# A hybrid decoder layer on one core: where the squares of rows stand in ScalarE's queue, which pool the first four weight chunks land in, and when the x rows by token are loaded

## The chip, the core and the metric

The kernel runs on one core of a Trainium2 chip. The metric is the device time of one execution in microseconds, as the median of several runs; lower is better. One further execution was recorded by the hardware profiler, and all single durations below are from that recording.

## The reference

One decoder layer over 256 tokens of width 2048, all in float32, with 256 memory tokens beside it:

```python
hn = rmsnorm(h, norm_mix_w)
q, k, v, g_ret, xr, yr, g_a, g_b = split(hn @ w_in)          # 2048 x 14336
ret_out = silu(g_ret) * head_groupnorm(chunkwise_retention(rotary(q), rotary(k), v))
rnn_out = gelu(yr) * rg_lru(causal_dwconv(xr))
merged = sigmoid(g_a) * (ret_out @ w_proj_ret) + sigmoid(g_b) * (rnn_out @ w_proj_rnn)
h = h + merged @ w_mix_out
mem_n = rmsnorm(mem, norm_mem_w)
h = h + memory_cross_attention(rmsnorm(h, norm_xa_w), mem_n, xa_w_q, xa_w_k, xa_w_v, xa_w_o)
h = h + conv_gated_ffn(rmsnorm(h, norm_ffn_w), ffn_w_up, ffn_w_down)   # width 5632
return rmsnorm(h, final_norm_w)
```

Each rmsnorm needs, for each token, the sum of squares over the 2048 features. The change concerns three of these sums (of x, of the memory rows, of h after each of the two residual additions) and the loads at the very start.

## The kernel before, in words

**Products.** Every weight matrix is cut into blocks of 512 columns, and each block into chunks of 4 row tiles of 128 (1 MB in float32); the first two blocks, of q and of v, are cut into chunks of 2, 2, 4, 4 and 4 row tiles that alternate (chunk 0 of q, chunk 1 of v, chunk 2 of q, and so on). Weights and activations are split into a rounded part `hi` and the rest `lo`, and a product is the sum of three matmuls. A full chunk takes 24 matmuls of 128x512; a chunk of `steps_t` has some of 128x256.

**The weight stream.** `weight_stream` lists all chunks in the order of use. `prefetch` (L233) takes them in that order, up to `AHEAD` = 2 chunks before their use: it issues the load of `raw` on SP's queue (L249), then for each half of the chunk a cast to `hi` on ScalarE, ACT in the profile (L276), and a subtraction to `lo` on VectorE, DVE (L277). `raw` has 3 buffers, `hi` and `lo` 6 each, that is three chunks. Chunks 0 and 1 are loaded in four single row tiles together, chunks 2 to 5 in pieces of two row tiles (512 KB), which I call 4a and 4b for chunk 4; later ones in one piece. Beside the first five chunks of q the transposed x comes in pairs of row tiles (`xt`, 256 KB a pair, L530), which `split_cols` scales and splits on ACT and DVE (L451, L452). x by token (`nat`, four loads of 512 KB, L228) is used for the sums of squares alone (L493), two rows when chunk 8 is taken and two at chunk 9.

**The order of work.** Most instructions are put into each engine's queue by a scheduler that works from priorities in program order; matmuls keep the program's order. Each queue then runs strictly in order. `later(n, fn)` puts a piece of code n + 1 chunks later in the program. Of SP's loads at most eight are under way at once: each waits for the landing of the eighth before it, besides what its buffer waits for.

**The big pool.** All larger tiles (rows, planes, splits, gates) take one of 27 buffers of 4 KB a partition, in turn, from `big`.

**Turning rows.** `by_dma` turns rows by token into rows by feature: two copies of half words into `pl` on ACT (L385), two DMA transposes on SP's queue into `pt` (L387), and, some chunks later, `join`: two copies from `pt` into `f` on ACT (L396), and what follows from `f`.

**The residual.** `residual` (L840) runs after `w_mix_out` and after `xa_w_o`. It makes four products (0 to 3), of four chunks each. The first three chunks of products 0 and 1 come first, then the last chunk of 0, the last of 1, and then products 2 and 3 whole. After each product, DVE adds it to the rows of h (L852), `squares` sums the squares of the new rows on ACT in two instructions (L867), and `by_dma` turns the rows; `turn` then splits `f` by `split_cols`. In the first residual, `memory_steps` hangs other work between the products: at block 1 the squares of the memory rows, `mnat` (four loads of 512 features each, two instructions a load, L493), and what makes `rsms` of them; at block 3 the loads of the transposed memory. The merged rows that feed the first residual are turned by the same `by_dma`; the join of the last of them comes four chunks after its gate product.

Of the kernel before, what the change touches and what calls it, by code (L numbers as in the profile page):

```python
# [9 lines left out]
F32 = mybir.dt.float32  # L10
# [7 lines left out]
P = 128  # L18
# [10 lines left out]
BW = 512  # L29
KC = 4  # L30
KH = 2
RAW_BUFS = 3
# [106 lines left out]
def hybrid_layer(  # L139
# [19 lines left out]
    wp = ctx.enter_context(tc.tile_pool(name="wp", bufs=2))  # L159
# [8 lines left out]
    def nm(s):  # L168
        count[0] += 1
        return f"{s}_{count[0]}"  # L170

    def big(shape, dt=F32, s="b"):
        return bp.tile(shape, dt, tag="big", name=nm(s))
# [11 lines left out]
    def load_rows(src, c, cs=slice(0, BW), t=None):  # L185

        if t is None:
            t = big([P, 2, BW], s="nat")
        rows = src[0].rearrange("(t p) d -> p t d", p=P)
        sp.dma_start(out=t[:, :, cs], in_=rows[:, :, c * BW + cs.start : c * BW + cs.stop])  # L190
        return t
# [31 lines left out]
    def load_x(n):  # L223
        while len(xin) < n:
            t = big([P, 2, BW], s="nat")
            rows = x[0].rearrange("(t p) d -> p t d", p=P)
            c = len(xin) * BW
            sp.dma_start(out=t, in_=rows[:, :, c : c + BW])  # L228
            xin.append(t)
# [3 lines left out]
    def prefetch(n):  # L233
        while len(ahead) < n and taken[0] < len(stream):
            i = taken[0]
            name, row, nk, c = stream[i]
            taken[0] += 1
            size = nk * P * BW
            src = wall[at[0] : at[0] + size].rearrange("(p k n) -> p k n", p=P, k=nk)
            at[0] += size  # L240
            raw = wp.tile([P, KC, BW], F32, tag="raw", bufs=RAW_BUFS, name=nm("raw"))
            k2 = row // (KH * P)
            early = i < 2 * len(EARLY)
            own = early and i % 2 == 0
            cuts = range(nk + 1) if i < 2 else range(0, nk + 1, KH) if i < 6 else (0, nk)
            if own:
                xs.load(k2 + 1)
            for a, b in zip(cuts, cuts[1:]):
                sp.dma_start(out=raw[:, a:b, :], in_=src[:, a:b, :])  # L249
                if i == 0 and a == 0:  # L250
                    sp.dma_start(out=xs.rest[0], in_=xs.rest[1])
                elif own and a == 0:
                    xs.load(k2 + nk // KH)
            if i >= 5:
                load_x(min(4, i - 4))
            if i == 8:
                sp.dma_start(out=cid, in_=consts[:, 0:C_DEC])
                sp.dma_start(out=pa[:, 16:P], in_=by_feature[:, 16:P])
                sp.dma_start(out=pb, in_=by_feature[:, P : P + 80])
            if i == 13:  # L260
                sp.dma_start(out=pf.rearrange("p a n -> p (a n)"), in_=by_feature[:, P + 80 :])
            if i in (8, 9):
                for b in (2 * i - 16, 2 * i - 15):
                    sum_squares(xin[b], ss0, b, pin=True)
            parts = []
            for k in range(0, nk, KH):
                if own:
                    xs[k2 + k // KH]
                hi = wp.tile([P, KH, BW], F32R, tag="hi", bufs=PART_BUFS, name=nm("hi"))
                lo = wp.tile([P, KH, BW], F32R, tag="lo", bufs=PART_BUFS, name=nm("lo"))  # L270
                for cs in (slice(k, k + 1), slice(k + 1, k + 2)) if i < 2 else (slice(k, k + KH),):
                    ds = slice(cs.start - k, cs.stop - k)
                    if i == 0:
                        dve.tensor_copy(hi[:, ds], raw[:, cs, :])  # L274
                    else:
                        act.copy(hi[:, ds], raw[:, cs, :])  # L276
                    dve.tensor_tensor(  # L277
                        out=lo[:, ds], in0=raw[:, cs, :], in1=hi[:, ds].bitcast(F32), op=ALU.subtract
                    )
                parts.append((hi, lo))  # L280
            ahead.append(((row, c), parts))
# [3 lines left out]
    def later(n, fn):  # L285

        pending.append((step[0] + n + 1, fn))
# [18 lines left out]
    def ended(steps):  # L306

        for a in steps:
            pass
        return a  # L310
# [41 lines left out]
    def steps_n(w, row, st, nk, col):  # L352

        a = acc()
        for k0, n, parts in chunks(nk, w, row, col):
            for tt in range(2):
                for kk in range(n):
                    k = k0 + kk
                    hi, lo = (t[:, kk % KH, :] for t in parts[kk // KH])
                    products_n(a[:, tt, :], st[k // 2][:, k % 2, :], hi, lo, tt, k == 0, k == nk - 1)  # L360
                if tt == 0 and isinstance(st, Pairs):
                    st[min(NT, k0 + 3 * n) // 2 - 1]
            yield a
# [13 lines left out]
    def by_dma(rows, then, wait=1):  # L377


        planes = big([P, 2, 2, BW], U16, s="pl")  # L380
        turned_ = big([P, 2, 4, S], U16, s="pt")
        words = rows.bitcast(U16).rearrange("p t (n h) -> p h t n", h=2)
        with tc.high_priority(FREE):
            for h in range(2):
                act.copy(planes[:, :, h, :], words[:, h])  # L385
        for tt in range(2):
            sp.dma_start_transpose(  # L387
                out=turned_.rearrange("p h f s -> p (h f) s")[:, :, tt * P : (tt + 1) * P],
                in_=planes[:, tt].rearrange("p h n -> p (h n)"),
            )  # L390

        def join():
            f = big([P, 4, S], s="f")
            halves_ = f.bitcast(U16).rearrange("p f (s h) -> p h f s", h=2)
            for h in range(2):
                act.copy(halves_[:, h], turned_[:, h])  # L396
            then(f)

        later(wait, join)
# [89 lines left out]
    def sum_squares(rows, ss, c, pin=False):  # L489

        for tt in range(2):
            junk = tp.tile([P, BW], F32, tag="tmp", name=nm("junk"))
            i = act.activation(junk, rows[:, tt, :], AF.Square, accum_out=ss[:, tt, c : c + 1])  # L493
            if pin:
                tc.keep_in_program_order(i)

    def sums():
        return sp_.tile([P, 2, 4], F32, tag="ss0", name=nm("ss"))

    def rstd_rows(ss):  # L500

        var = sp_.tile([P, 2], F32, tag="var", name=nm("var"))
        dve.tensor_reduce(out=var, in_=ss, axis=AX.X, op=ALU.add)
        return rsqrt_small(var, 2, 1.0 / D, EPS)
# [3 lines left out]
    def rsqrt_small(ap, n, scale, eps):  # L508
        v = sp_.tile([P, n], F32, tag="rv", bufs=4, name=nm("rv"))
        dve.tensor_scalar(out=v, in0=ap, scalar1=scale, scalar2=eps, op0=ALU.mult, op1=ALU.add)  # L510
        o = sp_.tile([P, n], F32, tag="ro", bufs=5, name=nm("ro"))
        pool.tensor_tensor(out=o, in0=v, in1=mhalf[:, 0:n], op=ALU.pow)
        return o
# [158 lines left out]
    for g in range(2):  # L672
        dec = big([P, 4, S], s="dec")
        vs, turned = [], ([], [])
        for b, o in enumerate((O_Q, O_K)):
# [6 lines left out]
            if b == 1:  # L682
                sp.dma_start(
                    out=dec,
# [151 lines left out]
    hrow = [load_rows(x, c) for c in range(4)]  # L836
    mnat = [load_rows(mem, c) for c in range(4)]
    ms = Pairs(mem_t, p_mem, 3)

    def residual(w, st, out, wcol, steps=None):  # L840

        ss = sums()
        products = [steps_n(w, 0, st, NT, b * BW) for b in range(4)]
        for b in range(4):
            if steps:
                steps(b)
            if b == 0:
                for one in products[:2]:
                    for _ in range(NT // KC - 1):
                        next(one)  # L850
            h = hrow[b]
            dve.tensor_add(h, h, ended(products[b]))  # L852
            squares(h, ss, b)
            by_dma(hrow[b], lambda f, b=b: turn(f, b, out, wcol))
        return ss

    def turn(f, b, out, wcol):
        for pr in range(2):
            out.append(split_cols(f[:, 2 * pr : 2 * pr + 2, :], lambda j: wcol(4 * b + 2 * pr + j)))

    def squares(y, ss, i):
        for tt in range(2):
            square(y[:, tt, :], ss[:, tt, i : i + 1])
# [5 lines left out]
    rsms = []  # L869

    def memory_steps(b):
        if b == 1:
            ss = sums()
            for c in range(4):
                sum_squares(mnat[c], ss, c)
            rsms.append(rstd_rows(ss))
        if b == 3:
            ms.load(2)
            for k2 in range(4):
                later(k2, lambda k2=k2: ms[k2])  # L880
# [175 lines left out]
    for kind, b, *n in ff_plan():  # L1056
# [6 lines left out]
        else:  # L1063
            final = b + n[0] == NF // 4
            if final:
                wfin = []
                for i in range(2):
                    t = big([P, 2, BW], s="wf")
                    sp.dma_start(
                        out=t.rearrange("p a n -> p (a n)"),  # L1070
# [37 lines left out]
```

## Time and profile before

| | |
|---|---|
| median of 3 runs | 2016.69 us (2016.46 to 2019.35) |
| the profiled execution's own time | 2016.58 us |
| span of its instructions | 2014.5 us |
| TensorE matmuls (PE) busy | 1999.1 us, 99% of the span |
| VectorE (DVE), ScalarE (ACT) busy | 1263.5 us (63%), 1247.8 us (62%) |
| mean granted TensorE clock | 0.997 |
| DMA | 423.02 MB, mean 210 GB/s |
| chain of waits that ended last | PE 96%, the others 1% or less each |

How to read it: PE is the matmuls of TensorE and PEld its weight loads; SPq is SP's queue, which only issues DMAs. In the timeline, a line has its start and length in us from the span's start, the engine, the line of the kernel, the operation, what it writes `<-` what it reads, and how many were merged into the line; the bracket is the idle time of the engine before it and what ended that. Matmuls are pipelined, so one shows 0.39 us and follows the one before by 0.23.

### The profile page before, as it was taken

To read this page: it belongs to the slowest core of one execution; us is meant where nothing else is said; L and a number is where in the kernel's file an instruction comes from. 1 tells how busy PE (TensorE), PEld (TensorE's weight loads), DVE (VectorE), ACT (ScalarE), POOL (GpSimd) and SP (SyncE) were. 2 spreads that over 40 slices of the span, in tenths; PEclk is the share of its full clock that TensorE was granted. 3 is DMA by queue.
4 is the path that set the end of the run, shared out by engine and by line. 5 is a ranking of instruction groups with operands and counts; after the bars stand their busy time and mean duration, and the time that the engine had idled before them with its cause. 6 is when DMAs were issued, how large, how long until landed. Compare 5 with 4: busy or idle time off the path is not lost.

```text
span 2014.5 us, 23604 instructions
## 1 busy us (share of the span) xinstructions
PE 1999.1 (99%) x9044; PEld 1664.3 (83%) x9044; DVE 1263.5 (63%) x1563; ACT 1247.8 (62%) x1506; POOL 7.7 (0%) x12
## 2 busy tenths in 40 slices
PE   9999999999999999999999999999999999999998
PEld 7888888888888888878888888888888888888887
DVE  5867757888545555456555555566775577664675
ACT  5556648888444455487675656766763466744763
POOL 0000000000000000000000000000000000000000
PEclk9999999999999999999999999999999999999999
DMA  8755757665555566767766645767665566655663
GB/s 299 233 210 172 235 199 196 235 206 188 209 190 192 195 207 211 260 227 241 227 208 205 197 176 184 217 205 215 214 223 216 195 191 217 232 210 200 208 230 125
DMA packets 189376, 423.02 MB, mean 210 GB/s; under 512 B 131664, under 2 KB 136400, under 8 KB 144208
## 3 DMA queue, kind: packets, MB, share of 16 engines
q1 hardware_dynamic: 188832, 421.00, 63.5%
q8 instruction: 70, 1.15, 0.2%
q10 hardware_dynamic: 432, 0.53, 0.1%
q14 instruction: 42, 0.34, 0.0%
HBM read 388.46 MB, written 2.10 MB: 194 GB/s over the span
## 4 chain that ended last, share of the span: by engine, by line
PE 96%; DMA 1%; ACT 1%; issue 1%; DVE 1%; SPq 0%; POOLq 0%; POOL 0%; ACTq 0%; DVEq 0%
PE acc L214 94%; PE sm L214 3%; DMA raw<-in_wall 1%; DMA pt<-pl 1%; DVE lo L277 0%; ACT pl L385 0%; ACT hi L276 0%; ACT f L396 0%; ACT junk L867 0%; DVE nat L852 0%; ACT s L451 0%; SPq L249 0%; ACT nat L1042 0%; DVE s L452 0%; SPq L387 0%
## 5 line engine op out<-in xcount | busy, mean ns | idle before, releaser
L214 PE MATMUL acc<-hi,s 128*128 128x512 f32 (+1 forms) x5680 | 1739.9, 388 | 3.0 <-ACT hi L276 2.5
L277 DVE TENSOR_TENSOR lo<-raw,hi 128x1024 fp32r<-128x1024 f32 (+1 forms) x714 | 859.4, 1218 | 645.9 <-ACT hi L276 629.5
L214 PEld LDWEIGHTS acc<-hi,s 128*128 128x128 f32 x5680 | 1062.4, 188 | 220.1 <-ACT hi L276 2.9
L214 PE MATMUL acc<-lo,s 128*128 128x512 f32 (+1 forms) x2840 | 1100.6, 388 | 0.5 <-DVE lo L277 0.5
L276 ACT CAST hi<-raw 128x1024 fp32r<-128x1024 f32 (+1 forms) x712 | 733.0, 1048 | 497.5 <-PE acc L214 428.1
L214 PEld LDWEIGHTS acc<-lo,s 128*128 128x128 f32 x2840 | 533.7, 188 | 110.1 <-DVE lo L277 1.0
L396 ACT COPY f<-pt 128x1024 uint16<-128x1024 uint16 x118 | 151.4, 1349 | 85.0 <-DMA pt<-pl 85.0
L385 ACT COPY pl<-rows 128x1024 uint16<-128x1024 uint16 x90 | 89.7, 1044 | 64.5 <-DVE rows L409 55.8
L409 DVE TENSOR_SCALAR rows<-acc,ro 128x512 f32<-128x512 f32 x68 | 47.7, 742 | 3.1 <-PE acc L214 3.1
L965 DVE SCALAR_TENSOR_TENSOR fv<-f,pf,fv 128x255 f32<-128x255 f32 (+1 forms) x88 | 35.8, 477 | 0.7 <-ACT fv L963 0.7
L965 DVE SCALAR_TENSOR_TENSOR fg<-f,pf,fg 128x255 f32<-128x255 f32 (+1 forms) x88 | 35.6, 477 | 0.0
L452 DVE SCALAR_TENSOR_TENSOR s<-f,pb,s 128x256 fp32r<-128x256 f32 x48 | 20.1, 478 | 6.6 <-ACT s L451 6.6
L963 ACT ACTIVATE fv<-f,pf 128x256 f32<-128x256 f32 x44 | 22.9, 592 | 0.0
L963 ACT ACTIVATE fg<-f,pf 128x256 f32<-128x256 f32 x44 | 22.8, 591 | 0.0
L428 ACT ACTIVATE s<-fo 128x512 fp32r<-128x512 f32 x22 | 13.6, 633 | 14.2 <-DVE fo L985 14.2
L777 DVE SCALAR_TENSOR_TENSOR xr<-f,pa,xr 128x255 f32<-128x255 f32 (+2 forms) x48 | 19.9, 478 | 3.1 <-ACT xr L775 3.0
L451 ACT ACTIVATE s<-f,pb 128x256 fp32r<-128x256 f32 x48 | 20.6, 498 | 0.0
L385 ACT COPY pl<-nat 128x1024 uint16<-128x1024 uint16 x16 | 15.9, 1042 | 6.9 <-DVE nat L852 6.9
L214 PEld LDWEIGHTS sm<-s,s 128*128 128x128 f32 x144 | 18.8, 191 | 0.9
L214 PE MATMUL sm<-s,s 128*128 128x256 f32 (+1 forms) x144 | 18.6, 279 | 0.0
L214 PE MATMUL acc<-s,hi 128*128 128x512 f32 x64 | 17.4, 410 | 0.4 <-DVE hi L274 0.3
L440 ACT ACTIVATE v<-acc,ro 128x512 fp32r<-128x512 f32 x16 | 10.9, 683 | 7.7 <-DVE v L441 7.7
(152 smaller groups left out, 625.5 us busy)
## 6 DMA issues: line engine op xcount, KB each, us to landing
raw<-in_wall SPq DMA_DIRECT2D x352, 1024.0 KB, 4.8
nat<-in_x SPq DMA_DIRECT2D x8, 512.0 KB, 7.8
raw<-in_wall SPq DMA_DIRECT2D x6, 512.0 KB, 6.8
nat<-in_mem SPq DMA_DIRECT2D x4, 512.0 KB, 9.3
xt<-in_mem_t SPq DMA_DIRECT2D x8, 256.0 KB, 3.6
pt<-pl SPq DMA_TRANSPOSE x118, 4.1
xt<-in_x_t SPq DMA_DIRECT2D x7, 256.0 KB, 8.2
out<-nat SPq DMA_DIRECT2D x6, 256.0 KB, 2.8
```

Of the source, the lines that this page charges most:

```text
L214: tc.keep_in_program_order(pe.matmul(*a, **k))
L276: act.copy(hi[:, ds], raw[:, cs, :])
L277: dve.tensor_tensor(out=lo[:, ds], in0=raw[:, cs, :], in1=hi[:, ds].bitcast(F32), op=ALU.subtract)
L385: act.copy(planes[:, :, h, :], words[:, h])
L396: act.copy(halves_[:, h], turned_[:, h])
L409: dve.tensor_scalar_mul(rows[:, tt, :], a[:, tt, :], r[:, tt : tt + 1])
L428: act.mul(t[:, :, 0:S], src, scale)
L451: act.activation(t[:, j, 0:S], src[:, j, :], AF.Identity, scale=wcol(j))
L452: dve.scalar_tensor_tensor(out=t[:, j, S:BW], in0=src[:, j, :], scalar=wcol(j), in1=t[:, j, 0:S].bitcast(F32), op0=ALU.mult, op1=ALU.subtract,
L777: dve.scalar_tensor_tensor(out=y[:, s:S], in0=z[:, 0 : S - s], scalar=p_cw(3 - s, t), in1=y[:, s:S], op0=ALU.mult, op1=ALU.add,)
L963: act.activation(y, z[:, j, :], AF.Identity, scale=pf[:, 2, t : t + 1], bias=pf[:, 3, t : t + 1])
L965: dve.scalar_tensor_tensor(out=y[:, s:S], in0=z[:, j, 0 : S - s], scalar=pf[:, 2 - s, t : t + 1], in1=y[:, s:S], op0=ALU.mult, op1=ALU.add,)
```

## The change

It has three parts. First, the raw weights of chunks 0 to 3 land in big buffers and not in the three of `raw`. Second, x by token is issued one load after chunk 6 and two more after chunk 7, where it was one after each of chunks 5, 6 and 7; the last stays after chunk 8. Third, the sums of squares: in the first residual the squares of the memory rows are no longer all at block 1; they are hung on the chunks from block 0 on, one load of 512 features a chunk, and the sum's root on the chunk after. In both residuals `by_dma` comes ahead of the squares in the program; the squares of blocks 0 and 1 come 3 and 4 chunks later, and the join of block 1 one chunk later than it did.

```diff
@@ prefetch
-            raw = wp.tile([P, KC, BW], F32, tag="raw", bufs=RAW_BUFS, name=nm("raw"))
+            if i < 4:
+                raw = big([P, KH, BW], s="raw")
+            else:
+                raw = wp.tile([P, KC, BW], F32, tag="raw", bufs=RAW_BUFS, name=nm("raw"))
...
-            if i >= 5:
-                load_x(min(4, i - 4))
+            if i >= 6:
+                load_x(min(4, 2 * i - 11))
@@ residual
             h = hrow[b]
             dve.tensor_add(h, h, ended(products[b]))
-            squares(h, ss, b)
-            by_dma(hrow[b], lambda f, b=b: turn(f, b, out, wcol))
+            by_dma(h, lambda f, b=b: turn(f, b, out, wcol), 1 + (b == 1))
+            if b < 2:
+                later(2 + b, lambda h=h, b=b: squares(h, ss, b))
+            else:
+                squares(h, ss, b)
@@ memory_steps
-        if b == 1:
+        if b == 0:
             ss = sums()
             for c in range(4):
-                sum_squares(mnat[c], ss, c)
-            rsms.append(rstd_rows(ss))
+                later(c, lambda c=c: sum_squares(mnat[c], ss, c))
+            later(4, lambda: rsms.append(rstd_rows(ss)))
```

In the built program TensorE's instructions and their order are the same. On SP, ACT and DVE the order differs in two places, the first nine chunks and the first residual, and on ACT in a third, small one: in the second residual one of block 0's two squares stands behind the two casts that it stood ahead of.

## The prediction, made before the changed kernel ran

> **What bounds the kernel now.** I read the page first. Its first table says that TensorE works nearly the whole span, so a change that adds no matmul can win only where TensorE waits or where its clock falls.
>
> ```profile
> PE 1999.1 (99%) x9044; PEld 1664.3 (83%) x9044; DVE 1263.5 (63%) x1563; ACT 1247.8 (62%) x1506; POOL 7.7 (0%) x12
> ```
>
> The timeline of TensorE lists its waits in brackets. Before 8 us there are four short ones, 0.7 us together. After that there are only these five:
>
> ```profile
> 18.33 0.50 PE L214 MATMUL acc<-s,lo 128*128 128x256 f32 x2 [0.99 <-DVE lo L277]
> 20.27 2.62 PE L214 MATMUL acc<-s,lo 128*128 128x256 f32 x14 [1.44 <-DVE lo L277]
> ...
> 880.37 0.73 PE L214 MATMUL acc<-hi,s 128*128 128x512 f32 x2 [2.48 <-ACT hi L276]
> 881.63 0.79 PE L214 MATMUL acc<-lo,s 128*128 128x512 f32 x1 [0.53 <-DVE lo L277]
> ...
> 1303.98 0.50 PE L214 MATMUL acc<-hi,s 128*128 128x512 f32 x1 [0.48 <-DVE s L452]
> ```
>
> The table by stretches, cut at the edges of the clock's records, gives what follows a wait (columns: us, busy time of PE, PEld, DVE, ACT, POOL, granted clock, DMA share, GB/s):
>
> ```profile
> 17.79:21.21 3.42, 1.44 (x10) 1.24 (x10) 3.29 (x5) 2.78 (x4) 0.00 (x0) 1.00 1.05 411
> 21.21:24.62 3.41, 3.41 (x14) 3.02 (x13) 2.48 (x4) 1.30 (x3) 0.00 (x0) 0.50 1.01 402
> ...
> 877.95:881.37 3.42, 0.73 (x2) 0.30 (x2) 1.51 (x2) 3.42 (x7) 0.00 (x0) 1.00 0.53 102
> 881.37:884.78 3.41, 3.15 (x8) 2.48 (x8) 3.41 (x4) 3.41 (x4) 0.00 (x0) 0.50 0.51 109
> ```
>
> A stretch of 3.4 us in which TensorE was busy 1.44 or 0.73 us is each time followed by 3.4 us at half clock, in which 1.7 us of work is lost. So the early wait costs more than its idle time. The last matmul of chunk 3 starts at 16.96; at 0.23 us a matmul chunk 4 could start at 17.19, take 5.45 (24 x 0.227) and let chunk 5 start at 22.64. Chunk 5 starts at 27.27: 4.6 us lost. In the first residual block (products counted from 0), the third chunk of product 2 could start at 877.73 and starts at 880.37; two chunks later the addition at L852 for block 2 starts at 893.88 where 888.87 was possible: 5.0 us lost.
>
> Why chunk 4 waits is told by SP's timeline and two landings (DMA list, one issue each, last column us to landing):
>
> ```profile
> 4.02 3.94 SPq L249 DMA_DIRECT2D raw<-in_wall  x2
> 8.00 0.43 SPq L530 DMA_DIRECT2D xt<-in_x_t  x1
> 9.29 0.33 SPq L249 DMA_DIRECT2D raw<-in_wall  x1
> ```
>
> ```profile
> raw<-in_wall SPq DMA_DIRECT2D x1, 512.0 KB, 6.7
> raw<-in_wall SPq DMA_DIRECT2D x1, 512.0 KB, 7.8
> ```
>
> With three raw buffers, chunk 3 is issued at 7.63 and chunk 4's first half at 9.29, each after a lo subtraction of chunk 0 or 1; its second half, at 10.13, lands at 17.89, and 2.38 us later (cast, subtraction) TensorE goes on. The queue ran dry meanwhile: 177 GB/s at 12 to 14 us, a mean of 404 from 14 to 40.
>
> Why the residual waits stands in ACT's timeline:
>
> ```profile
> 865.39 0.63 ACT L867 ACTIVATE junk<-nat 128x512 f32<-128x512 f32 x1
> ...
> 866.63 0.62 ACT L493 ACTIVATE junk<-nat 128x512 f32<-128x512 f32 x1
> ...
> 870.92 0.62 ACT L493 ACTIVATE junk<-nat 128x512 f32<-128x512 f32 x1
> ...
> 872.14 2.55 ACT L396 COPY f<-pt 128x1024 uint16<-128x1024 uint16 x2 [0.51 <-DMA pt<-pl]
> ...
> 879.29 3.87 ACT L276 CAST hi<-raw 128x1024 fp32r<-128x1024 f32 x4
> ```
>
> The cast that TensorE waits for at 880.37 has its raw weights since 861.79 (issue 857.03, 4.8 to landing) and a free hi buffer from about 865.6 and 867.0 (product 1 ends then; three chunks of hi are held). It stands behind ten squares, two joins f, four column splits and two plane copies.
>
> **The start.** After the change the first four chunks take big buffers, so up to raw of chunk 7 no load waits for a subtraction, only for the eighth DMA before it (SP's order with its waits). That is never the limit here: chunk 4's second half waits for chunk 1's first, landed at 6.82. Up to chunk 2's raw (4.02 + 5.9 = 9.95) nothing changes. Behind it, in the new order, stand the second x_t pair (256 KB), chunk 3 (512), chunk 4a (512), x_t (256), chunk 4b (512). In the full queue chunks 4b, 5a and 5b landed at 17.89, 19.18 and 20.45, so 512 KB take 1.28 us and 256 KB 0.64. The landings become 10.6, 11.9, 13.2, 13.8 and 15.1 (now 12.4, 11.5, 15.95, 16.6, 17.89). ACT is free for each cast. DVE sets the end: lo of chunk 2 to 12.29 as now, then in the new order the x_t pair 0.87, lo3 1.23, lo4a 1.23, pair 0.87, lo4b 1.23: 13.2, 14.4, 15.6, 16.5, 17.7. Chunk 3 needs its lo at 14.9 (now ready 13.84): 0.5 us of cover left, past which each us costs one. Chunk 4 runs two matmuls from 17.19 and waits from 17.42 to 17.76, 0.3 us instead of 2.8; the stretch of the clock stays nearly full, so half clock should not come. Chunk 5 starts at 17.76 + 5.45 - 0.23 = 22.98: **gain 4.3 us**, at most 4.6. At least, if the loads land no faster than now, nothing; I take the full queue's pace, since the loads in question are the same rows of the same tensors.
>
> The x rows by token are issued later in order (the first after x_t of chunk 6, two after chunk 7). They feed the squares, the first of which runs at 33.41; the last x load keeps its place behind chunk 8. The reader on TensorE is the small product at 49.44, POOL's part done by 42: about 6 us of cover, and the whole queue moves up some 3 us. Cost nothing; without cover, one for one. SP itself issues as many DMAs as before.
>
> **The residual after w_mix_out.** The memory rows' squares (8 x 0.615 = 4.9 us of ACT) move ahead by some 23 us, one block of 512 features a chunk. In the new order of ACT they stand about the join f of the last merged block, at 840.6 now, and wait for the memory rows, issued 835.24 to 836.93 and landing 8.1 to 11.5 us later, at 843.4 to 848.5. Replayed from ACT's rows (square pair 1.23, half join 1.3, split 0.57): 843.4 squares, 844.6 f, squares of blocks 1 and 2 to 848.4, f, one of block 3's, the two splits to 851.4, last square 852.0. The next cast began at 851.06 when its raw landed; now at 852.0, its lo at 854.3. TensorE needs that chunk at 856.0, when the addition's chunk before it ends. So 1.0 us is spent and 2.1 remain. ACT idled there for 6.69 us.
>
> Block 0's square halves and block 1's are now queued around the cast: planes to 865.5, one square 866.0, hi 866.0 to 868.1, squares to 869.9, first hi of the next chunk from 871.0, f when pt lands at 872.1 to 874.7, second hi to 875.7. So the chunk TensorE wants at 877.73 is ready by 870.7 with its lo (subtractions from 868.3, behind block 1's addition), and the one wanted at 883.2 by 877. The wait and the half clock go: **gain 5.0 us**.
>
> What is late next: block 1's planes still end at 878.9. Two raw loads are now ahead of its transposes on SP (one after lo at 870.7, one at 877.0), so its pt lands as block 0's did behind a load, 5.3 to 5.7 us after issue and not 3.2: 883.8. The join, put one chunk later, ends at 886.4 and the second hi of product 3's second chunk at 887.4, its lo by 888.7; TensorE wants it at 894.1. Five us of cover. Were it gone, each us would cost one.
>
> In the residual after xa_w_o only one square of block 0 changes place with two casts; there TensorE does not wait. The 0.48 at 1303.98 follows block 3's join, whose order is the same: it stays.
>
> **Sum.** 4.3 + 5.0 = 9.3 us, from the profiled execution's 2016.58 (span 2014.5 and 2.1 around it; the median of the runs is 2016.69, 0.1 more): 2007.3. A measurement of this kernel can tell about 0.2%, 4 us, from no change.
>
> **The clock, by the skill.** Both half-clock stretches here follow stretches busy 42% and 21%, with idle gaps of 2.5 us at most. The Trainium skill, page TensorE: Matmul & The Clock Gate, Part 1, says the clock is halved after at least one idle window of about 3.4 us, and sets the rule "no PE-idle gaps >~3.4µs"; by that no gap here is long enough and the halving would have another cause that stays, and the sum would be 5.8 and not 9.3. The trace disagrees on the gap's length and agrees on the window (3.413 us).
>
> **Rivals.** (1) The early loads land no earlier: the engines share their rate among all that is issued, and chunk 4's halves gain less than 2.8 us. For it speaks that packets of the first 9 us moved only 230 to 340 GB/s; against it that landings keep the order of issue. With the residual's gain alone: 2011.6, between that and 2007.3 if half is won.
> (2) The half clock stays in both places, for a reason other than the idle share; only idle time goes: 2.5 + 3.3 = 5.8, 2010.8. Against it: in all the span only these two stretches are at half clock before the end.
> (3) The residual's wait moves to a later cast, behind a join whose transposes land late. It needs more than 5 us on top of 5.7; no landing of a pt row near it shows that. 2012.3.
> (4) Slower: ACT runs in order, so if the memory rows land late, their squares at 843 hold up f, the splits and every cast behind. Slack is 1.2 us at the last block's square and 2.1 at TensorE, 3.3 in all; past that one for one, and 1.7 for the clock. To be slower than now, 7.6 us of stall plus clock must eat 9.3: rows 11 us late, at 859.4. At 15 us late: 2016.58 - 9.3 + 11.7 + 1.7 = 2020.7. The rows sit in SP's order as before, which speaks against it.
>
> **How the numbers follow.** Both gains 0.65 (2006.0 to 2009); (1) 0.17; (2) 0.05; (3) 0.07; (4) 0.04; other losses 0.02. The range takes the first, most of (1) and (2): 2006.0, the highest gain 4.6 + 5.0 and the 0.48 with 0.4 of scatter, to 2011.8. Faster by over 0.2%: the first, nearly all of (1), (2): 0.85; within: (3) and leftovers 0.09; slower, (4) and other losses, 0.06.
>
> **What would show it.** Right: chunk 4's second cast near 15.1, no half clock at 21 us, chunk 5 at about 23; near 873 (all 4.3 earlier) no wait of PE on ACT hi and no half clock; 1303.98's wait alone left. Wrong: chunk 4b landing at 17 or later; PE waiting for the chunk of 856; a new wait on hi or lo within 40 us after the residual's second product.

## The result, and the profile after

The changed kernel takes 2011.14 us (median of 8 runs, 2008.91 to 2013.62), the kernel before 2016.58 in runs beside it (8 runs, 2014.03 to 2019.35). The ratio is 0.9972, with a 95% interval of 0.9962 to 0.9981: 5.4 us are gained where 9.3 were forecast. The two profiled executions lie further apart, 2016.58 against 2008.91, or 7.7 us. Both differences have to be explained: the profile shows where the 7.7 come from, and the experiments show why a usual pair of runs differs by less.

From the page of the kernel after, the busy times. Its lines of code stand 3 lower than before in the places named here: `hi` L279, `lo` L280, column splits L454 and L455, planes L388, join L399, addition L855, squares of the memory rows L496; the squares of the residual stand 6 lower, at L873.

```profile
PE 1995.5 (99%) x9044; PEld 1661.7 (83%) x9044; DVE 1264.2 (63%) x1563; ACT 1248.7 (62%) x1506; POOL 7.7 (0%) x12
```

TensorE is busy 3.6 us less with the same 9044 matmuls. Nearly all of it is the half clock: two stretches at 1.7 us are 3.4. From the timeline of TensorE, every wait over 0.3 us after the first 8 us, and the first product of chunk 5:

```profile
11.36 0.96 PE L214 MATMUL acc<-s,hi 128*128 128x512 f32 x3 [0.35 <-ACT hi L279]
...
17.81 0.85 PE L214 MATMUL acc<-s,lo 128*128 128x256 f32 x5 [0.37 <-DVE lo L280]
...
23.23 0.62 PE L214 MATMUL acc<-hi,s 128*128 128x512 f32 x2
...
919.08 0.50 PE L214 MATMUL acc<-hi,s 128*128 128x512 f32 x1 [1.27 <-DVE s L455]
...
1296.55 0.50 PE L214 MATMUL acc<-hi,s 128*128 128x512 f32 x1 [0.37 <-DVE s L455]
```

Before, chunk 4 waited 0.99 and 1.44 us and chunk 5 started at 27.27; now one wait of 0.37 us is left and chunk 5 starts at 23.23. The waits of 2.48 and 0.53 us in the first residual are gone. The wait of 1.27 us at 919 is new. The table by stretches (columns as before) shows that the clock stays whole where it was halved:

```profile
17.54:20.95 3.41, 3.14 (x20) 2.90 (x21) 3.22 (x5) 2.16 (x4) 0.00 (x0) 1.00 1.00 404
20.95:24.36 3.41, 3.41 (x16) 2.81 (x15) 2.29 (x5) 2.80 (x4) 0.00 (x0) 1.00 1.05 412
...
850.00:880.00 30.00, 30.00 (x134) 24.85 (x133) 20.38 (x21) 23.07 (x31) 0.00 (x0) 1.00 0.78 247
```

The start works as forecast. SP's timeline and the landing of chunk 4b (DMA list, the issue at 6.94 alone) say why:

```profile
6.94 2.41 SPq L252 DMA_DIRECT2D raw<-in_wall  x3
10.25 0.33 SPq L533 DMA_DIRECT2D xt<-in_x_t  x1
```

```profile
raw<-in_wall SPq DMA_DIRECT2D x1, 512.0 KB, 8.5
```

Three loads are issued in a row from 6.94, the first of them 4b, which was issued at 10.13 before. It lands at 15.4 and not at 17.89. From 12 to 14 us the transfers now move 414 GB/s (177 before).

ACT's timeline in the first residual, the rows that the replay named:

```profile
839.38 0.63 ACT L496 ACTIVATE junk<-nat 128x512 f32<-128x512 f32 x1 [2.69 <-DMA nat<-in_mem]
...
847.76 3.88 ACT L279 CAST hi<-raw 128x1024 fp32r<-128x1024 f32 x4
...
862.16 1.98 ACT L279 CAST hi<-raw 128x1024 fp32r<-128x1024 f32 x2
...
868.47 2.56 ACT L399 COPY f<-pt 128x1024 uint16<-128x1024 uint16 x2 [0.24 <-DMA pt<-pl]
...
880.28 2.56 ACT L399 COPY f<-pt 128x1024 uint16<-128x1024 uint16 x2 [1.49 <-DMA pt<-pl]
```

With the start's 4.04 us added back these are 843.42, 851.80, 866.20, 872.51 and 884.32; the replay had 843.4, 852.0, 866.0, 872.1 and 883.8.

**Where the time went, by TensorE's progress.** Its instructions have the same order in all these kernels, so the start of one and the same matmul can be compared across traces. I take five marks: chunk 5's first product, and the matmuls that start at 850.11, 890.00 and 930.10 us in the profile after, and 1290.12 to 1310.06. Between the marks that I leave out (chunk 5 to 850, 930 to 1290) the traces of the table take the same 826.88 and 360.03 us, and from 1310 to the last matmul 688.99 us except in one. So a trace is described by four numbers (us, all worked out from the starts of these matmuls; the kernels are explained below):

| trace | chunk 5 starts | 850 to 890 | 890 to 930 | 1290 to 1310 |
|---|---|---|---|---|
| before | 27.27 | 44.97 | 38.31 | 20.05 |
| after | 23.23 | 39.89 | 40.09 | 19.93 |
| after, once more (e_whole) | 24.15 | 39.89 | 42.31 | 20.63 |
| start alone (e_start) | 23.57 | 46.03 | 38.31 | 19.83 |
| residual alone (e_resid) | 24.90 | 39.89 | 40.25 | 20.57 |
| memory rows' squares alone (e_memsq) | 26.15 | 39.89 | 40.75 | 20.79 |
| residual blocks' squares alone (e_later) | 26.95 | 39.89 | 40.41 | 21.01 |
| two chunks in the big pool (e_raw2) | 23.69 | 39.89 | 40.17 | 20.78 |
| early splits (e_fix) | 23.95 | 39.89 | 38.31 | 21.34 |
| later join (e_j3) | 23.00 | 39.89 | 38.31 | 20.37 |
| both (e_j3f) | 23.52 | 39.89 | 38.31 | 20.17 |

Before against after: 4.04 + 5.08 - 1.78 + 0.12 = 7.46 us, and the last matmul starts 7.44 us earlier. Both forecast gains are there (4.3 and 5.0 forecast), and 1.8 us are given back at a place that the prediction did not name.

### The profile page after: what moved, and what is told of

It is laid out like the page before. It is cut to its first block, busy times and chain, and to the rows that moved or that the text cites. A ratio compares the mean times of both kernels' runs of the same rounds, so it can differ in the third digit from the quotient of the medians.

```text
span 2007.1 us, 23602 instructions
## 1 busy us (share of the span) xinstructions
PE 1995.5 (99%) x9044; PEld 1661.7 (83%) x9044; DVE 1264.2 (63%) x1563; ACT 1248.7 (62%) x1506; POOL 7.7 (0%) x12
## 4 chain that ended last, share of the span: by engine, by line
PE 97%; DMA 1%; issue 1%; DVE 0%; ACT 0%; SPq 0%; POOLq 0%; POOL 0%; DVEq 0%; ACTq 0%
PE acc L214 95%; PE sm L214 3%; DMA raw<-in_wall 0%; DMA pt<-pl 0%; DVE lo L280 0%; SPq L252 0%; DVE s L455 0%; SPq L533 0%; ACT f L399 0%; ACT nat L1048 0%; ACT junk L873 0%; DVE nat L855 0%; ACT pl L388 0%; ACT hi L279 0%; POOLq L1110 0%
## 5 line engine op out<-in xcount | busy, mean ns | idle before, releaser
L280 DVE TENSOR_TENSOR lo<-raw,hi 128x1024 fp32r<-128x1024 f32 (+1 forms) x714 | 860.2, 1219 | 645.5 <-ACT hi L279 628.6
L279 ACT CAST hi<-raw 128x1024 fp32r<-128x1024 f32 (+1 forms) x712 | 733.7, 1048 | 500.2 <-PE acc L214 433.7
L399 ACT COPY f<-pt 128x1024 uint16<-128x1024 uint16 x118 | 151.5, 1348 | 76.4 <-DMA pt<-pl 76.4
L388 ACT COPY pl<-rows 128x1024 uint16<-128x1024 uint16 x90 | 89.7, 1044 | 63.8 <-DVE rows L412 55.9
L455 DVE SCALAR_TENSOR_TENSOR s<-f,pb,s 128x256 fp32r<-128x256 f32 x48 | 20.1, 479 | 4.7 <-ACT s L454 4.7
L388 ACT COPY pl<-nat 128x1024 uint16<-128x1024 uint16 x16 | 15.9, 1042 | 8.6 <-DVE nat L855 8.6
L454 ACT ACTIVATE s<-f,pb 128x256 fp32r<-128x256 f32 x48 | 20.6, 498 | 0.0
```

What stands on the lines that cost most here:

```text
L280: dve.tensor_tensor(out=lo[:, ds], in0=raw[:, cs, :], in1=hi[:, ds].bitcast(F32), op=ALU.subtract)
L454: act.activation(t[:, j, 0:S], src[:, j, :], AF.Identity, scale=wcol(j))
L455: dve.scalar_tensor_tensor(out=t[:, j, S:BW], in0=src[:, j, :], scalar=wcol(j), in1=t[:, j, 0:S].bitcast(F32), op0=ALU.mult, op1=ALU.subtract,
```

## The experiments

The first four ran on one chip, beside 27 runs of the kernel before with a median of 2015.88 us. The runs e_raw2, e_memsq, e_later, e_gap and e_gap2 are single ones, on another chip beside one run of the kernel before of 2014.29 us; their traces are read, and their times decide nothing.

**The kernel after, once more (e_whole).** No edit.

> The whole change again, to see what varies. Theory 1 (waits and half clock): TensorE shows the same waits as in the first profile of it, 0.37 us at chunk 4, one of 1 to 2.5 us near 918 us behind the splits of the transposed memory, 0.4 us near 1296; where the one near 918 is longer than about 1.7 us, half clock follows it and the execution is 1.7 us longer. 5 to 8 us below before. Theory 2 (scatter has nothing to do with the waits): the waits are the same to 0.1 us and the time differs all the same.

Measured: 2010.69 us (11 runs, 2009.08 to 2016.11), ratio 0.9975 (0.9967 to 0.9984). Its profiled execution took 2012.72 us and shows what the first one did not: the new wait can bring half clock with it.

```profile
918.81 0.50 PE L214 MATMUL acc<-hi,s 128*128 128x512 f32 x1 [0.53 <-ACT s L454]
920.60 0.50 PE L214 MATMUL acc<-hi,s 128*128 128x512 f32 x1 [1.29 <-DVE s L455]
```

```profile
917.74:921.15 3.41, 1.60 (x6) 0.79 (x5) 3.41 (x6) 3.41 (x7) 0.00 (x0) 1.00 1.10 246
921.15:924.57 3.42, 3.42 (x9) 2.64 (x8) 3.23 (x5) 1.60 (x4) 0.00 (x0) 0.50 1.04 344
```

The first fence is TensorE's timeline, the second the table by stretches: 1.82 us of waiting lie in one stretch of the clock's records, TensorE is busy 1.60 of 3.41 us in it, and the next stretch is at half clock. The stretch from 890 to 930 takes 4.0 us more than the 38.31 of before. The wait of 0.37 us at chunk 4 is not there: TensorE reaches whole clock only at 9.8 us (3.9 in the first trace) and comes to chunk 4 late by itself.

**The start alone (e_start).** The kernel before with this part of the diff:

```diff
+            if i < 4:
+                raw = big([P, KH, BW], s="raw")
...
-            if i >= 5:
-                load_x(min(4, i - 4))
+            if i >= 6:
+                load_x(min(4, 2 * i - 11))
```

> Only the start is changed: raw weights of chunks 0 to 3 in the big pool, x by token later; the residual is as before. Theory 1: 4.0 us below before (chunk 5 starts near 23.2 and not 27.3), no half clock near 21 us; the wait of 2.5 + 0.5 us and the half clock stay in the residual, some 4 us earlier than before. Rival (the gain at the start is lost again to a wait for later loads): less than 1 us below before, with a new wait between 23 and 60 us.

Measured: 2012.99 us (11 runs), ratio 0.9988 (0.998 to 0.9997): 2.9 us gained, where 4.0 were expected. Chunk 5 starts at 23.57, there is no half clock at 21 us and no wait near 918. The old wait in the residual is there, and in this trace it is followed by two half stretches, where the first profile had one:

```profile
873.08:876.49 3.41, 1.11 (x5) 0.57 (x4) 0.73 (x2) 3.41 (x6) 0.00 (x0) 1.00 0.18 35
876.49:879.91 3.42, 3.17 (x7) 2.07 (x8) 3.23 (x3) 3.42 (x5) 0.00 (x0) 0.50 0.63 118
879.91:883.32 3.41, 3.41 (x10) 2.65 (x9) 1.84 (x3) 3.41 (x5) 0.00 (x0) 0.50 0.88 327
```

**The residual alone (e_resid).** The kernel before with the other parts of the diff, in `residual` and `memory_steps`.

> Only the squares are changed (both residuals and the memory's); the start is as before. Theory 1: the wait and the half clock near 880 go, 5.0 us, and the new wait for the splits of the transposed memory costs 1.3 back: 3.7 us below before. The two waits at chunk 4 and the half clock near 21 us stay. Rival (the new wait comes from the shift that the start makes): no wait near 922, 5.0 below.

Measured: 2013.58 us (11 runs), ratio 0.9986 (0.9974 to 0.9997): 2.3 us gained, where 3.7 were expected. The residual's wait is gone, and the new wait is here (1.27 us before 920.87), so it belongs to this part. The old wait of chunk 4 is there too, but against the expectation it brings no half clock in this trace, and chunk 5 starts at 24.90 and not at 27.27:

```profile
17.41 0.50 PE L214 MATMUL acc<-s,lo 128*128 128x256 f32 x2 [0.49 <-DVE lo L277]
19.47 1.93 PE L214 MATMUL acc<-s,lo 128*128 128x256 f32 x14 [1.56 <-DVE lo L277]
```

```profile
15.51:18.92 3.41, 1.92 (x9) 1.13 (x7) 2.75 (x4) 2.88 (x5) 0.00 (x0) 1.00 1.02 397
18.92:22.34 3.42, 2.87 (x19) 2.70 (x20) 3.08 (x4) 2.33 (x4) 0.00 (x0) 1.00 1.04 419
```

The 1.56 us are cut in two by the edge of a stretch at 18.92, and neither stretch is empty enough. The two parts alone give 2.9 + 2.3 = 5.2 us, which is what the whole gives here (2015.88 - 2010.69). So nothing shows that they interfere; but by the intervals each part is known to no better than about 2 us.

**The splits ahead of the planes (e_fix).** In the kernel after, the splits of pairs 4 and 5 of the transposed memory, which TensorE waits for at 919, are put ahead of block 3's planes:

```diff
         if b == 3:
             ms.load(2)
-            for k2 in range(4):
-                later(k2, lambda k2=k2: ms[k2])
+            for k2 in range(6):
+                later(min(k2, 3), lambda k2=k2: ms[k2])
```

> The whole change, and the splits of the transposed memory's pairs 4 and 5 asked for three chunks ahead of their use in the program, so that they stand ahead of the last block's planes in ScalarE's queue. Theory 1: the wait near 918 us goes, 1.3 us below the whole change, more where that wait brings half clock. Rival (the wait only passes to the next thing that the chunk needs): as the whole change, with a wait for hi, lo or another pair within 15 us of 918.

Measured: 2008.19 us (5 runs, 2007.08 to 2009.42), ratio 0.9961 (0.9947 to 0.9974). By medians that is 2.5 us below the whole change (2010.69), where 1.3 or more were expected. The wait near 918 is gone, and 890 to 930 is back at 38.31. The table from 910 to 925 us, the kernel after first, then e_fix:

```profile
910.00:925.00 15.00, 13.72 (x60) 10.87 (x59) 11.16 (x18) 11.59 (x20) 0.70 (x1) 1.00 0.91 299
```

```profile
910.00:925.00 15.00, 15.00 (x68) 12.43 (x67) 11.48 (x20) 14.32 (x24) 0.69 (x1) 1.00 0.74 222
```

Near 1296 there are now two waits of 0.76 and 0.75 us.

**Only two chunks in the big pool (e_raw2).** The kernel after with `if i < 2:` in place of `if i < 4:`.

> The kernel after with only the first two chunks' raw weights in the big pool, not four. If the start's gain comes from chunk 4's loads, which no longer wait for casts of the first chunks: with two chunks in the big pool the three buffers of the other pool serve chunks 2, 3 and 4, chunk 4's loads are issued as early, only those of chunk 5 and on come later, so chunk 5's first product starts within 0.3 us of the kernel after's 23.23 us and the start costs the same. If all four are needed: chunk 5 lands later than its product asks, with a PE wait of 0.5 us or more between 23 and 40 us.

Measured: one run, 2014.09 us. Chunk 5 starts at 23.69, 0.46 us after the first profile of the kernel after, where 0.3 were expected, but within the 23.00 to 24.15 that the other traces with the new start show, and no wait follows to 40 us. So in this trace two chunks carry the start's gain. The run's time has another reason: from 1310 us to the end it takes 692.6 and not 689.0 us, for two waits that no other profile has, at a place where its instructions are those of the kernel after:

```profile
1415.41 0.50 PE L214 MATMUL acc<-lo,s 128*128 128x512 f32 x1 [1.36 <-DVE lo L280]
...
1504.39 0.50 PE L214 MATMUL acc<-lo,s 128*128 128x512 f32 x1 [1.55 <-DVE lo L280]
```

The first follows a DMA transpose that landed 4.8 us after issue (3.2 in the kernel after). Why it was late this run does not show.

**One edit of the residual at a time (e_memsq, e_later).** The kernel before with the squares of the memory rows spread alone, and with the squares of the residual blocks put off alone:

```diff
 e_memsq
-        if b == 1:
+        if b == 0:
...
-                sum_squares(mnat[c], ss, c)
+                later(c, lambda c=c: sum_squares(mnat[c], ss, c))
...
 e_later
-            squares(h, ss, b)
+            if b < 2:
+                later(2 + b, lambda h=h, b=b: squares(h, ss, b))
+            else:
+                squares(h, ss, b)
...
```

> The kernel before with the memory rows' squares alone moved (one block for each step of the first residual, from block 0 on); start, residual blocks' squares and join as before. Theory: the wait on hi at 873 came from four squares of memory rows that ACT did in one piece ahead of the cast; spread, they do it no harm, so the wait at 873 (1.9 to 2.5 us) is gone with this edit alone, and the new wait near 918 comes (1.0 to 1.8 us), since the transposed memory's splits stand behind the same work. Rival: the residual blocks' own squares hold the cast, and the wait at 873 stays over 1 us. Start as before (27.3 us at chunk 5, with a half clock or without). Span 2009 to 2013 us.

> The kernel before with only the residual blocks' squares put off (blocks 0 and 1 by two and three steps); the memory rows' squares in one piece at block 1, the join and the start as before. Theory: as ACT's order is filled by due times, this edit alone too takes the wait at 873 away, since the cast goes ahead of what is put off; the wait near 918 comes here too if it belongs to the splits of the transposed memory behind block 3's planes. Rival: the memory squares in one piece hold the cast, and the wait at 873 stays over 1 us. Start as before. Span 2009 to 2013 us.

Measured: one run each, 2015.10 and 2014.92 us. The table by stretches, e_memsq first:

```profile
850.00:880.00 30.00, 30.00 (x135) 24.82 (x133) 20.10 (x23) 24.99 (x35) 0.70 (x1) 1.00 0.74 261
```

```profile
850.00:880.00 30.00, 30.00 (x134) 24.86 (x133) 18.34 (x20) 24.80 (x38) 0.69 (x1) 1.00 0.77 263
```

Either edit alone takes the whole wait away: in both traces the memory rows' squares now run from 842 to 851 us, in ACT's idle time. So in e_later it is the scheduler that moved them, though their place in the program did not change. Neither is needed for the other. In both the new wait comes (0.59 and 1.28 us in e_memsq, 0.25 and 1.28 in e_later), with the join of block 1 where it was before: it does not come from the diff's later join. Both starts show the old wait with half clock; that is the larger part of what makes these spans (2011.5 and 2012.3 us) longer than the 2009.5 of e_resid.

**The clock by itself (e_gap, e_gap2).** The kernel after with the first cast of some chunks repeated, so that TensorE waits in quiet places (the edit of e_gap; e_gap2 has nine chunks, 4 to 9 times each):

```diff
-                        act.copy(hi[:, ds], raw[:, cs, :])
+                        for _ in range({108: 10, 117: 11, 126: 12, 135: 13}.get(i, 1) if k == 0 else 1):
+                            act.copy(hi[:, ds], raw[:, cs, :])
```

> The kernel after, with the first cast of four chunks of the stream (cast near 601, 650, 699 and 750 us) repeated 10, 11, 12 and 13 times, so that PE waits in four quiet places for growing times, by estimate 0.8 to 4 us (each repeat is 0.94 us of ACT; the cast is some 11 us ahead of its product). It measures what makes the half clock, by itself. Theory of shares: PE's time falls into windows of 3.41 us that run freely, and a window in which PE is busy less than about half is followed by one of half clock (47% busy was, 56% was not), so waits under 1.5 us are never followed by it, waits of 1.7 to 3.4 us only where they fall mostly into one window, and a wait split between two windows may cost nothing. Rival, the length alone: half clock follows every wait over about 2.3 us, wherever it falls. Rival, the whole idle window: none below 3.4 us. The time is longer than the kernel after's by the waits and 1.7 us for each stretch of half clock: by 5 to 15 us.

> The kernel after with repeated casts at nine chunks of the stream (cast near 402, 453, 507, 552, 601, 651, 699, 750 and 797 us; 8, 8, 8, 8, 9, 8, 4, 7 and 8 times), so that PE waits some 2 us at the last five of them (by the waits of 2.9, 5.0, 9.4 and 7.7 us that 10, 11, 12 and 13 casts made at 601, 651, 699 and 750 us, less 0.94 us for each cast left out), and for a time that no run has shown at the first four. Theory of shares: a 3.41 us window of whole clock in which PE is busy under about half (47% was followed by half clock, 54% was not) is followed by half clock, any other is not, so among waits of some 2 us those that lie in one window are followed by it (busy share 40 to 46%), those split between two are not. Rival, the length: all waits of over about 2.2 us are followed by it and all under 1.7 us are not, however they are split. Time: the waits' sum (10 to 20 us) and 1.7 us for each stretch of half clock above the kernel after's.

Measured: 2044.41 and 2043.79 us, one run each, some 33 us above the kernel after, where 5 to 15 were expected of e_gap. The waits missed the estimate. In e_gap they were 2.9, 5.0, 9.4 and 7.7 us. In e_gap2 three of the first four were long (6.2, 6.6 and 3.1 us), and at the last five hardly anything was left, nothing over 0.6 us in one piece. So these runs show the two ends and not the middle. Two stretches of e_gap2:

```profile
536.64:540.06 3.42, 1.23 (x6) 0.69 (x4) 1.22 (x1) 3.36 (x5) 0.00 (x0) 1.00 0.00 0
540.06:543.47 3.41, 2.50 (x5) 1.59 (x6) 2.56 (x3) 1.77 (x2) 0.00 (x0) 0.50 0.00 0
...
949.66:953.07 3.41, 1.86 (x7) 0.96 (x6) 2.63 (x4) 3.41 (x7) 0.70 (x1) 1.00 1.07 277
953.07:956.50 3.43, 3.14 (x14) 2.60 (x15) 3.43 (x6) 1.82 (x3) 0.00 (x0) 1.00 1.11 308
```

The second pair is the new wait of the kernel after, 0.57 and 1.27 us here, and no half clock follows it. With the waits of the other traces these fit one rule for whole clock. I cut all the traces into stretches of 3.413 us from the edge of their clock's records and take TensorE's busy share in each that a wait touches:

| | busy share of a stretch at whole clock |
|---|---|
| the next is at half clock | 0% (four), 21%, 27%, 33%, 36%, 36%, 42%, 42%, 44%, 47% |
| the next is at whole clock | 54%, 55%, 55%, 56%, 61%, 61%, 61%, 62% and all above |

No trace breaks the order; between 47% and 54% there is none to tell. The length alone does not decide: 0.53 + 1.29 us in one stretch (e_whole) was followed by half clock, 0.49 + 1.56 us over two (e_resid) was not. A wholly idle stretch is not needed either.

**The later join (e_j3), and both repairs (e_j3f).** The first is the kernel after with one number changed, the second is e_fix with it:

```diff
-            by_dma(h, lambda f, b=b: turn(f, b, out, wcol), 1 + (b == 1))
+            by_dma(h, lambda f, b=b: turn(f, b, out, wcol), 1 + 3 * (b == 1))
```

> The kernel after with one number changed: the join of block 1 in both residuals comes two chunks later still (1 + 3 * (b == 1)), so that on VectorE the addition for block 2 stands ahead of block 1's column splits, not behind them. Theory of the chain: counted from the same product of TensorE, the addition for block 2 runs 2.8 us later in the kernel after than before (it stands behind block 1's splits, whose transposes land when they did), and with it the planes, the transposes, the loads of the transposed memory behind them, their splits and the addition for block 3; so here the addition for block 2 is 2 to 3 us earlier, the wait near 918 shrinks from 1.3 us and more to under 0.5 us, and the median falls by 1 to 2 us to 2009 to 2010 us. Rival, the order alone: the splits of pairs 4 and 5 stand behind block 3's planes and squares here too, block 3's addition comes when its product ends and no earlier, and the wait stays over 1 us.

> The kernel after with both: the join of block 1 two chunks later, and the splits of all six first pairs of the transposed memory ahead of block 3's planes. If the two take the same wait away, it is no faster than the better one of them alone, 2008 to 2009 us; if the later join also takes away the waits near 1296 us (1.5 us in the kernel with the early splits alone), since in the second residual too the addition for block 2 no longer stands behind block 1's splits, up to 1.5 us less, 2006.5 to 2008 us.

Measured, beside 9 runs of the kernel before with a median of 2017.24: e_j3 2008.04 us (5 runs, 2007.06 to 2010.96), ratio 0.9957 (0.9943 to 0.997); e_j3f 2007.66 us (5 runs, 2007.22 to 2007.86), ratio 0.9952 (0.9939 to 0.9964). The chain is read from DVE's timelines. Before, the addition for block 2 (L852) comes after 1.09 us of idle time, as soon as its product ends, and block 1's splits are long done:

```profile
887.71 1.67 DVE L452 SCALAR_TENSOR_TENSOR s<-f,pb,s 128x256 fp32r<-128x256 f32 x4
889.29 3.49 DVE L277 TENSOR_TENSOR lo<-raw,hi 128x1024 fp32r<-128x1024 f32 x3
893.88 1.22 DVE L852 TENSOR_TENSOR nat<-nat,acc 128x1024 f32<-128x1024 f32 x1 [1.09 <-PE acc L214]
```

After, it stands without a pause behind block 1's splits, and those behind the join that waited 1.49 us for its transposes:

```profile
883.78 1.23 DVE L280 TENSOR_TENSOR lo<-raw,hi 128x1024 fp32r<-128x1024 f32 x1 [3.73 <-ACT hi L279]
884.92 1.67 DVE L455 SCALAR_TENSOR_TENSOR s<-f,pb,s 128x256 fp32r<-128x256 f32 x4
886.50 1.22 DVE L280 TENSOR_TENSOR lo<-raw,hi 128x1024 fp32r<-128x1024 f32 x1
887.64 1.22 DVE L855 TENSOR_TENSOR nat<-nat,acc 128x1024 f32<-128x1024 f32 x1
```

In e_j3, by DVE's timeline, then ACT's, then the table by stretches:

```profile
884.04 1.22 DVE L280 TENSOR_TENSOR lo<-raw,hi 128x1024 fp32r<-128x1024 f32 x1 [2.85 <-ACT hi L279]
885.18 1.21 DVE L855 TENSOR_TENSOR nat<-nat,acc 128x1024 f32<-128x1024 f32 x1
```

```profile
913.59 1.69 ACT L454 ACTIVATE s<-xt,pb 128x256 fp32r<-128x256 f32 x4
915.19 1.98 ACT L279 CAST hi<-raw 128x1024 fp32r<-128x1024 f32 x2
```

```profile
910.00:925.00 15.00, 15.00 (x68) 12.43 (x67) 10.19 (x18) 13.09 (x23) 0.70 (x1) 1.00 0.81 274
```

Counted from the matmul of 890.00, the addition for block 2 runs at -5.24 before, -2.36 after and -4.60 in e_j3; the first load of the transposed memory is issued at 0.69, 5.46 and 3.45; the addition for block 3 runs at 17.79, 20.48 and 19.42; the splits that TensorE waits for start on ACT at 24.06, 26.75 and 23.81. The wait is gone. But of the 2.94 us by which those splits come earlier only 1.06 come with block 3's addition, where the whole 2.69 (20.48 - 17.79) would come back if it hung on block 2's addition alone. The rest is that the scheduler, with the join later, puts the splits ahead of a chunk's two casts (2.0 us) and not behind them. So this run shows the join's part in the chain for 1.06 us, which by itself would leave some 0.2 of the wait of 1.27 us (an estimate, their difference), and does not show it for the rest. Both repairs together are hardly better than one: 0.4 us, and the runs overlap. All three repaired kernels beat the kernel before, and by their medians also the kernel after.

## Why the prediction was right and wrong

**The start: the mechanism was right, and its price holds for the profiled pair alone.** In the profiled pair it is 4.04 us against 4.3. The landings came 0.3 us later each than worked out (10.89, 12.19, 13.50, 14.13 and 15.42 for 10.6, 11.9, 13.2, 13.8 and 15.1), chunk 4 waited 0.37 us for 0.34, and the half clock at 21 us is gone. The mis-sized term is "4.6 us lost", which took half clock and one trace's landing for certain. With the old start, chunk 5 began at 27.27, 24.90, 26.15 and 26.95 us in four traces, 26.3 on average; with the new one at 23.00 to 24.15 in seven of the table's eleven, 23.6. The usual gain is about 2.7 us. Two things vary. Chunk 4b landed (issue plus time to landing in the DMA list) at 17.89, 17.09, 16.81 and 17.59 us with the old start, the latest of them in the first profile, and at 15.2 to 16.1 with the new. And chunk 5 began 9.3 to 9.4 us after that landing in the three old traces with half clock, but 7.8 us after it in the one without and in all of the new but e_whole, where TensorE was late by itself.

**The residual: right.** 5.08 us against 5.0. The replay of ACT's queue met the recorded times to 0.5 us, the wait and its half clock are gone, and 850 to 890 takes 39.89 us in all nine traces of the table that have either edit of the squares. The old order took 44.97 and 46.03. One reading is short: the late cast stood behind twelve squares, not ten, for two more follow at 874.56 and 878.67. By e_memsq it is enough that the eight of the memory rows go.

**"What is late next": this step failed.** It followed block 1's late turn to the join and the `hi` and `lo` behind it, found "five us of cover", and stopped there. The join's splits also stand on DVE, ahead of the addition for block 2. On that addition hang block 2's planes and transposes, on SP the loads of the transposed memory behind those, their splits, the addition for block 3, its planes, and the splits of pairs 4 and 5. The 5 us that TensorE lost had covered that chain; once TensorE was 5 us ahead, the chain was late by the end of it. The timeline of ACT shows that end in the kernel after, and DVE's rows follow at 918.55. e_fix shows that this end makes the wait; the beginning, from the join to the addition for block 3, is read from the timelines, and e_j3 bears it out for 1.06 us:

```profile
911.73 2.00 ACT L388 COPY pl<-nat 128x1024 uint16<-128x1024 uint16 x2 [1.83 <-DVE nat L855]
...
914.86 1.99 ACT L279 CAST hi<-raw 128x1024 fp32r<-128x1024 f32 x2
916.75 1.70 ACT L454 ACTIVATE s<-xt,pb 128x256 fp32r<-128x256 f32 x4
```

The wait cost 1.78 us in the pair, and 1.8 to 4.0, 2.4 on average, in the table's six traces with the new residual and no repair (1.2 and 2.4 in e_gap and e_gap2, which are not in the table). The list of what would show the forecast wrong missed it too: it looked for a wait on `hi` or `lo` within 40 us after the residual's second product, whose addition is at 863.00; the wait was on `s`, 55 us after it.

**"It stays", the wait of 0.48 us near 1304: nearly.** In the pair it is 0.11 us shorter. But 1290 to 1310 took 20.05 and 19.83 us with the old residual and 20.62 on average in those six traces: 0.7 us more. That the change makes them is not shown. The kernel after itself took 19.93 once and 20.63 once, and e_memsq took 20.79, though from 935 us on its trace has the order of the kernel before on every engine. In e_j3f it is 20.17.

**The sum.** By these means: 2.7 + 5.6 - 2.4 - 0.7 = 5.2 us, where 5.6 is the mean of the two old residuals less 39.89. Measured by medians: 5.4 and 5.2. The forecast of 9.3 made one execution's price of the two stalls the usual one, 1.6 us too much at the start, and left out 3.1 us (2.4 that come late next, and 0.7 whose cause is open); the residual itself was 0.6 better. That 2011.14 us still lies between 2006.0 and 2011.8 is luck: that upper part of the range was kept for rivals (1) and (2), and neither came. What brought the time there, a start worth less in most executions and a wait uncovered further on, is none of the prediction's rivals as they stand.

**The rivals.** (1) did not come: the loads land earlier, chunk 4b at 15.42 us and not at 17.89. (2) did not come either: the half clock goes with the waits in both places; that it is a matter of the idle share within a stretch, as the prediction held, is borne out by the table of shares. The Trainium skill, page TensorE: Matmul & The Clock Gate, Part 1, calls the window of 3413 ns free-running, not set anew when a kernel starts. The traces agree, with stretches of 3.413 us and whole clock from 3.9 us (after) to 9.8 us (e_whole). The Trainium skill's rule there that it takes an idle window or a gap over about 3.4 us is not what these traces show: 47% busy was enough. (3) A wait behind a join whose transposes land late is nearest to what happened, but by way of DVE, some 43 us further on, and for about a third of the price. (4) The memory rows' squares held up nothing: they ran from 839.38 to 847.8 and the casts behind them were in time.

## What to carry to other kernels

When a stall of the busiest engine is taken away, follow what the late work releases on every engine's queue (the additions, loads and splits behind it, and not only the tile that was waited for) until a chain ends that has more slack than the time won: the stall itself was that chain's cover. A stall seen in one trace has one execution's price; where a window of the clock can halve the speed after it, take the price with and without that. Moving the program place of one piece of work can make a scheduler move its neighbours: try each edit alone before keeping both.

## What the runs showed of the hardware

The records of TensorE's clock come in stretches of 3.413 us whose edges lie differently in each execution: of those at whole clock, 47% busy and less was followed by half clock, 54% and more was not. So a wait can cost 1.7 us more or not, by where the edge falls: the two waits on the splits of the transposed memory, 0.53 and 1.29 us in e_whole, were followed by half clock; the same two in e_gap2, 0.57 and 1.27 us, were not. At half clock it is less plain: another half stretch followed all shares up to 73% and once 93%, and none followed 86%, 92%, 95%, 99% and 100%. What decides there stays open.
